# Key loads between z's weights, gate weights two rooms on, five PSUM banks for the delta rule: one decoder layer on one core

## The chip, the core and the metric

The kernel runs on one core of a Trainium2 chip. The metric is device time in microseconds, the median of three runs: 2111.9 us before the change (2111.68 to 2111.97). In the profile PE is TensorE, DVE is VectorE, ACT is ScalarE, POOL is GpSimd and SP is the engine whose queue issues nearly all loads and stores here.

## The reference

One layer of a hybrid decoder, 1024 tokens of width 1024, all in float32:

```python
x = layer_norm(a * x + 0.5 * swiglu(x, ffn1_wg, ffn1_wu, ffn1_wd), ln1_g, ln1_b)
proj = x @ w_in                       # q, k, v, z, b, a of 4 delta heads; q, keys, values, gates of 8 NSA heads
o_gdn = gdn_mixer(...)                # short causal conv, silu, l2norm, gated delta rule, rms norm * silu(z)
o_nsa = nsa_mixer(...)                # compressed + selected (top 16 of 16 blocks of 64) + window (512) attention
x = layer_norm(a * x + concat(o_gdn, o_nsa) @ w_out, ln2_g, ln2_b)
x = layer_norm(a * x + 0.5 * swiglu(x, ffn2_wg, ffn2_wu, ffn2_wd), ln3_g, ln3_b)

swiglu = (silu(x @ wg) * (x @ wu)) @ wd      # hidden width 2816
```

## The kernel before

All float32 products are made of three matmuls: each operand is split into a high part (a cast on ScalarE, `wh`, `xh`) and a low part (a subtraction on VectorE, `wl`, `xl`), and high x high, high x low and low x high add up in one PSUM bank. A bank holds 128 x 512 values; there are eight.

The stages in order, with their times in the profile:

- First FFN, `hidden` (to about 430): gate and up weights come in pairs of 128-column blocks (`load`, L247 to L260: a megabyte per weight and pair, into a ring of three rooms, `wring`, L197). Each pair's two products, one of 1024 x 1024 by 256 each, are made by Strassen-like schemes of seven products of half size (`Unit`, `prep` casts a weight, `run` L299 multiplies). Pair 0 takes rooms 0 and 1, four tiles of x that are set aside (`xf`) take room 2. For pair 0 the work is written out by hand up to L540, and pair 1's weights are loaded at L520 within it. The hand-written order holds for VectorE, ScalarE and POOL (in the second FFN for TensorE too). Sums of weights are `st`; L526 and L527 add up pair 0's products and so free their banks.
- Down projection (430 to 655), L642, into two sets of four banks.
- `project`, which holds the PSUM pools `pps` (products) and `gps` (all of the delta rule's banks, `bank`, L1308). `ln_first` transposes the normed rows (L122, `tp`, in banks of `gps`) into `xh`, `xl`; then eight blocks of q, k and v follow, each with a product of two halves (L173, 24 matmuls per half) and a causal convolution (`conv_block`, ScalarE copies each half out of PSUM at L841). The first two blocks' first halves are made before their second halves.
- `nat_block` (L958) and beside it the generator `gdn_couple`, which prepares the delta rule for eight chunks of 128 tokens. Per chunk `front` transposes q and k (L1341, two banks), and `back` transposes `lb` (L1415), makes a decay (L1419, L1421) and two halves of k against k and q (L1434); VectorE reads `lb`'s bank at L1426 (`zb`), and the others at L1436 and L1437. Product matmuls of other blocks (L173) stand between.
- `gdn_run` (from about 907), then `attend`: tiles of sparse attention (L1752, L1753, L1689), with the generator `z_blocks` between them, which makes z's eight products (L1083) one piece at a time. Its weights `zw`, half a megabyte per half block, come through two buffers: when four of a block's eight steps are done, the load of the next block's half goes out (L1061). Within the first block, `z_blocks` also issues the loads of the second head group's keys, `ks`, for two branches (selected, window) and two halves (`nsa_keys`, L1655: two loads of 256 KB each).
- Second FFN (from about 1440) and its down projection.

Instructions that aren't under a hand-written order are placed by a scheduler that goes by the program's order, by data and by free buffers. A room, a bank or a buffer is free when its last reader is done. SP issues its queue in order; an issue that has to wait holds all behind it.

Of the kernel before, what the change touches and what calls it, by code (L numbers as in the profile page):

```python
# [9 lines left out]
F32 = mybir.dt.float32  # L10
F32R = mybir.dt.float32r
# [5 lines left out]
PSUM = bass.MemoryType.PSUM  # L17

P = 128
# [28 lines left out]
class Layer:  # L48
# [135 lines left out]
    def hidden(self, wg, wu, hd, cols, halves, rows, extra, jobs):  # L184
        nc, tc = self.nc, self.tc
        eng = mybir.EngineType
        h0, h1 = halves
        with ExitStack() as st:


            def pool(n, **kw):
                return st.enter_context(tc.tile_pool(name=n, reuse_waits="tile", **kw))
# [4 lines left out]
            wring = Ring(*[(pool(f"fw{i}", bufs=1), "wraw") for i in range(3)])  # L197
# [49 lines left out]
            def load(w, p, parts=1):  # L247
                raw = wring.tile([P, ND, 2 * P], F32, "wraw")
                src = w[:, 2 * p * P:2 * (p + 1) * P].rearrange("(k p) f -> p k f", p=P)
                n = ND // parts  # L250

                def part(i):
                    nc.sync.dma_start(raw[:, i * n:(i + 1) * n], src[:, i * n:(i + 1) * n])

                if parts == 1:
                    part(0)
                    return raw
                return raw, part
# [139 lines left out]
            with tc.manual_schedule(engines=engines):  # L398
# [86 lines left out]
                def ready(n, src, vals, between=None):  # L485

                    w = [g.prep(src(g))]
                    for kc in range(4):
                        put(n, kc, vals[kc])
                    if between is not None:  # L490
                        between()
                    return w + [v.prep(src(v))]

                def go(i, n, w, k=None):
                    for u, x in zip(both, w):
                        u.p[i] = u.run(x, n, k)
# [20 lines left out]
                room("t4", h0)  # L517
                go(4, "t4", ready("t4", lambda u: u.w22, T))

                nxt = Gate(load(wg, 1)), Up(load(wu, 1))  # L520
                n = nxt[0]
                for x, w in (("x11", n.w11), ("x21", n.w12)):
# [446 lines left out]
    def project(self, ln_g, ln_b, w_in, a_log, dt_bias, pos_k, pos_v, k_w1, k_w2, v_w1, v_w2, outer):  # L969
        tc = self.tc  # L970
        self.w_in = w_in
        self.qkvT = self.scratch("qkvT", [12, P, T])
        self.zT = self.scratch("zT", [4, P, T])
        self.qd = self.scratch("qd", [HQ, P, T])
        self.kd = self.scratch("kd", [2, 2, P, T])
        self.cd = self.scratch("cd", [2, P, T])
        self.od = self.scratch("od", [GH, P, T])
        self.gts = self.mid.tile([P, NT, 32], F32, name="gts")
        self.KC = self.mid.tile([P, 2, 2, DH], F32R, name="KC")
        self.VC = self.mid.tile([DH, 2, 2, DH], F32R, name="VC")  # L980
        with ExitStack() as st:

            p1, p2 = [st.enter_context(tc.tile_pool(name=f"pw{i}", bufs=1, reuse_waits="tile")) for i in range(2)]
            self.raws, self.his, self.los = Ring((p1, "r0"), (p1, "r1"), (p2, "r2")), Ring((p1, "h0"), (p2, "h1")), Ring((p1, "l0"), (p2, "l1"))
            self.sb = st.enter_context(tc.tile_pool(name="psb", bufs=1, reuse_waits="tile"))
            with ExitStack() as ps:
                self.ps = ps.enter_context(tc.tile_pool(name="pps", bufs=4, space=PSUM, reuse_waits="tile"))
                self.pg = ps.enter_context(tc.tile_pool(name="gps", bufs=4, space=PSUM, reuse_waits="tile"))
                ws = [self.weights(w_in, 4 * P)]
                with tc.tile_pool(name="ln", bufs=4, reuse_waits="tile") as lsb:  # L990
                    scale = self.ln_first(lsb, self.pg, ln_g, ln_b)

                    ws.append(self.weights(w_in, 5 * P))
                    pps = [self.product(self.ps, "pr", *w, halves=(0,)) for w in ws]
                    for w, pp in zip(ws, pps):
                        self.product(self.ps, "pr", *w, halves=(1,), ps=pp)
                    for t, b in enumerate((4, 5, 6, 7, 0, 1, 2, 3)):
                        self.conv_block(b, pps[t] if t < 2 else None)
                        scale(t)
                couple = self.gdn_couple(a_log, dt_bias)  # L1000
                self.nat_block(couple)
                for _ in couple:
                    pass
                with tc.tile_pool(name="gc", bufs=1, reuse_waits="tile") as c1, tc.tile_pool(name="gb", bufs=2, reuse_waits="tile") as gb:
                    self.gdn_run(c1, gb)
                self.c_block(0, C_KC)
                self.c_block(1, C_VC)
                self.k_block(0, C_KS)
                self.k_block(1, C_KW)
                self.KS = {}  # L1010
                for br in range(2):
                    for half in (1, 0):
                        self.nsa_keys(0, br, half, self.acc_tile(2 * half + br, [P, 2, 512], F32R))
                self.nsa_consts()
                self.q_block(0)
                self.q_block(1)
                finish = self.cmp_mlp(0, pos_k, k_w1, k_w2, False)
                self.q_block(2)
                finish()
                finish = self.cmp_mlp(1, pos_v, v_w1, v_w2, True)  # L1020
                self.q_block(3)
                finish()


    def attend(self):
        nc, tc = self.nc, self.tc
# [3 lines left out]
        with ExitStack() as st:  # L1030
# [17 lines left out]
            def load_w(u):  # L1048

                for i, x in enumerate((self.xh, self.xl)):  # L1050
                    x[u] = self.xp[2 * i + u].tile([P, ND, 512], F32R, name=("xh", "xl")[i])
                for k in (4, 6, 0, 2):
                    for i, x in enumerate((self.xh, self.xl)):
                        loads.append(lambda i=i, x=x[u], k=k: nc.sync.dma_start(
                            x[:, k:k + 2, :].bitcast(F32), self.wo[i, u, k:k + 2].rearrange("k p c -> p k c")))

            def z_blocks():

                def load(n, k):
                    w = op.tile([P, 2, 4, P], F32R, name="zw", tag=("oh", "ol")[k], bufs=1)  # L1060
                    nc.sync.dma_start(w.bitcast(F32), self.zw[n % 4][:, k].rearrange("p i (k f) -> p i k f", f=P))  # L1061
                    return w

                w = [load(0, k) for k in range(2)]

                def finish(u, b, pp):
                    z = zp.tile([P, 512], F32, name="z", padded_shape=[P, T])

                    def out():
                        nc.scalar.mul(z, z, self.nw)  # L1070
                        nc.sync.dma_start(self.zT[b][:, u * 512:u * 512 + 512], z)

                    return [lambda: nc.scalar.activation(z, pp, AF.Tanh), lambda: None,
                            lambda: nc.vector.scalar_tensor_tensor(z, z, 1.0, pp, op0=ALU.add, op1=ALU.mult), out]

                for n in range(8):
                    u, b = divmod(n, 4)
                    pp = self.zps.tile([P, 512], F32, name="pr")
                    for kc in range(ND):
                        h, l = [w[kc // 4][:, i, kc % 4] for i in range(2)]  # L1080
                        xh, xl = self.xh[u][:, kc, :], self.xl[u][:, kc, :]
                        for i, (a, x) in enumerate(((h, xh), (h, xl), (l, xh))):
                            nc.tensor.matmul(pp, a, x, start=(kc == 0 and i == 0), stop=(kc == ND - 1 and i == 2))  # L1083
                        if kc % 4 == 3 and n < 7:
                            w[kc // 4] = load(n + 1, kc // 4)
                        yield
                        if n == 0 and kc in (3, 5):
                            for br in range(2):
                                self.nsa_keys(1, br, kc // 5, nk.tile([P, 2, 512], F32R, name=f"ks{br}{kc // 5}"))
                    if b == 3:  # L1090
                        load_w(u)
                    for f in finish(u, b, pp):
                        f()
                        yield
# [125 lines left out]
            with tc.manual_schedule(engines={eng.PE}):  # L1220
# [7 lines left out]

                nxt = group(0)
                filler.append(z_blocks())  # L1230
                for t in reversed(range(NT)):
                    if t + 2 < NT:
# [634 lines left out]
```

## Time and profile before

| | us |
|---|---|
| median of three runs | 2111.9 |
| the profiled run | 2113.0 |
| its span | 2111.2 |
| TensorE busy | 2064.5 (98%) |
| VectorE busy | 1508.6 (71%) |
| ScalarE busy | 922.5 (44%) |
| POOL busy | 586.6 (28%) |

The span runs from the first to the last instruction of one profiled execution; the granted TensorE clock is 0.996 over it. Times of the trace are counted from the span's start. "Granted clock" is the share of 2.4 GHz that the throttle granted; 0.5 is 1.2 GHz. An engine's row "idle before" names what ended its idle time.

### The profile page before, as it was taken

The page shows a single profiled execution, that of the slowest core. Times are in us where ns is not written, and L with a number is a line of the kernel's source. Part 1 is how long each engine was busy: PE and PEld are TensorE (multiplying, and loading weights), DVE is VectorE, ACT ScalarE, POOL GpSimd, SP SyncE. Part 2 cuts the span into 40 slices and gives each one's busy share as a digit, 9 for nine tenths or more (in the row PEclk, how much of TensorE's full clock was granted, in tenths as well). Part 3 has the DMA queues.
Part 4 walks back from the last instruction along what each step waited for, and adds up shares of the span by engine and source line. Part 5 has one row for each costly group of instructions (what it writes and reads, how often), then busy time and mean ns, then how long its engine had stood idle before and what let it go on. Part 6 is the DMA issues. An engine that isn't in the chain of part 4 may idle for free.

```text
span 2111.2 us, 29640 instructions
## 1 busy us (share of the span) xinstructions
PE 2064.5 (98%) x10247; PEld 1707.3 (81%) x10247; DVE 1508.6 (71%) x2644; ACT 922.5 (44%) x1957; POOL 586.6 (28%) x608
## 2 busy tenths in 40 slices
PE   9999999999999999999999999999999999999998
PEld 7788888888888897788877777787788888887886
DVE  7876767688877747735556777766976566569998
ACT  6333333344443434244446766656433333334441
POOL 2544445200021113000013354452254453310011
PEclk9999999999999999999999999999999999999999
DMA  4345555198623724477554421222333233259751
GB/s 147 123 147 178 200 185 180 71 334 278 230 69 95 232 93 152 136 220 199 143 145 170 163 73 50 72 85 81 110 105 120 95 111 102 73 219 328 235 195 55
DMA packets 251384, 316.46 MB, mean 150 GB/s; under 512 B 25393, under 2 KB 154530, under 8 KB 251234
## 3 DMA queue, kind: packets, MB, share of 16 engines
q1 hardware_dynamic: 246498, 298.05, 43.6%
q0 software_dynamic: 4736, 16.52, 2.0%
q8 instruction: 81, 1.33, 0.3%
q14 instruction: 69, 0.57, 0.1%
HBM read 219.08 MB, written 93.32 MB: 148 GB/s over the span
## 4 chain that ended last, share of the span: by engine, by line
PE 79%; DVE 8%; DMA 4%; issue 3%; POOL 2%; ACT 2%; SPq 1%; POOLq 0%; DVEq 0%; ACTq 0%
PE bk L299 34%; PE dn L642 17%; PE pr L173 9%; PE pr L1125 3%; PE po L1689 3%; PE pt L1676 2%; PE pr L1083 2%; PE pr L958 1%; DMA raw<-h 1%; PE sc L1753 1%; PE sc L1752 1%; DVE wl L285 1%; PE ga L1528 1%; PE ga L1538 1%; DVE st L278 1%
## 5 line engine op out<-in xcount | busy, mean ns | idle before, releaser
L299 PE MATMUL bk<-x,wh 128*128 128x512 f32 x1040 | 321.4, 390 | 4.9 <-DVE ev L527 2.8
L642 PE MATMUL dn<-bl,ah 128*128 128x512 f32 x616 | 240.3, 390 | 1.5 <-DVE bl L103 1.5
L642 PE MATMUL dn<-bh,ah 128*128 128x512 f32 x616 | 240.0, 390 | 0.2 <-DVE ev L320 0.2
L642 PE MATMUL dn<-bh,al 128*128 128x512 f32 x616 | 239.8, 389 | 0.0
L299 PEld LDWEIGHTS bk<-x,wh 128*128 128x128 f32 x1040 | 194.4, 188 | 47.0 <-issue 4.1
L299 PE MATMUL bk<-t,wh 128*128 128x512 f32 x704 | 217.1, 389 | 0.3 <-DVE t L240 0.3
L299 PE MATMUL bk<-acc,wh 128*128 128x512 f32 x704 | 217.0, 389 | 0.4 <-ACT ev L233 0.2
L284 ACT CAST wh<-st 128x512 fp32r<-128x512 f32 x176 | 108.3, 622 | 239.0 <-PE bk L299 202.9
L299 PE MATMUL bk<-x,wl 128*128 128x512 f32 x520 | 202.6, 390 | 2.1 <-DVE wl L285 2.0
L100 ACT CAST ah<-raw 128x512 fp32r<-128x512 f32 x154 | 95.3, 622 | 175.5 <-PE dn L642 94.3
L356 POOL TENSOR_TENSOR ev<-ev 128x512 f32<-128x512 f32 x80 | 131.6, 1647 | 144.5 <-ACT wh L284 65.7
L284 ACT CAST wh<-wraw 128x512 fp32r<-128x512 f32 x130 | 80.2, 623 | 186.5 <-PE bk L299 172.3
L1786 POOL TENSOR_SCALAR pr<-pr,f 128x512 f32<-128x512 f32 (+3 forms) x192 | 108.1, 582 | 176.6 <-DMA ks<-kd 36.2
L299 PEld LDWEIGHTS bk<-t,wh 128*128 128x128 f32 x704 | 132.1, 188 | 28.2 <-DVE t L240 0.8
L1757 DVE TENSOR_REDUCE nm<-sc 128x1 f32<-128x512 f32 (+3 forms) x192 | 98.2, 517 | 79.3 <-PE sc L1755 75.1
L299 PEld LDWEIGHTS bk<-acc,wh 128*128 128x128 f32 x704 | 132.0, 188 | 28.2 <-ACT ev L233 0.4
L278 POOL TENSOR_TENSOR st<-wraw 128x512 f32<-128x512 f32 x76 | 100.9, 1328 | 183.0 <-DVE wl L285 153.8
L285 DVE TENSOR_TENSOR wl<-wraw,wh 128x512 fp32r<-128x512 f32 x130 | 117.4, 907 | 37.7 <-ACT wh L284 36.5
L1758 ACT ACTIVATE pr<-sc,nm 128x512 f32<-128x512 f32 (+3 forms) x192 | 106.3, 555 | 72.0 <-DVE nm L1757 63.9
L642 PEld LDWEIGHTS dn<-bl,ah 128*128 128x128 f32 x616 | 115.6, 188 | 26.9 <-DVE bl L103 3.6
L299 PE MATMUL bk<-t,wl 128*128 128x512 f32 x352 | 137.0, 389 | 0.0
L299 PE MATMUL bk<-acc,wl 128*128 128x512 f32 x352 | 136.9, 389 | 0.0
(398 smaller groups left out, 4793.7 us busy)
## 6 DMA issues: line engine op xcount, KB each, us to landing
raw<-h SPq DMA_DIRECT2D x154, 256.0 KB
raw<-in_ffn_wd_dram SPq DMA_DIRECT2D x154, 256.0 KB
h<-ev SPq DMA_DIRECT2D x140, 256.0 KB
wraw<-in_ffn_wg_dram SPq DMA_DIRECT2D x20, 1024.0 KB
wraw<-in_ffn_wu_dram SPq DMA_DIRECT2D x20, 1024.0 KB
wraw<-in_w_in_dram SPq DMA_DIRECT2D x20, 512.0 KB
acc<-in_x_dram SPq DMA_DIRECT2D x32, 256.0 KB
wo<-ev SPq DMA_DIRECT2D x32, 256.0 KB
```

The lines of the kernel that those rows point to most:

```text
L100: nc.scalar.copy(hi, src)
L173: nc.tensor.matmul(ps[half], ws[:, kc, :], xs[half][:, kc, :], start=(kc == 0 and i == 0), stop=(kc == ND - 1 and i == 2))
L278: (e or u.adder).tensor_tensor(t, a, b, op=o)
L284: nc.scalar.copy(h, src)
L285: u.low = nc.vector.tensor_tensor(l, src, h.bitcast(F32), op=ALU.subtract)
L299: nc.tensor.matmul(ps, w[:, kc, :], v[kc], start=(kc == 0 and i == 0), stop=(kc == 3 and i == 2))
L356: (nc.vector if u.f + 2 == NF else nc.gpsimd).tensor_tensor(t, t, u.gate.g[i, j], op=ALU.mult)
L642: nc.tensor.matmul(ps, a[:, t * P:(t + 1) * P], w, start=start and i == 0, stop=stop and i == 2)
L1125: nc.tensor.matmul(pp, a[:, kc, :], w[u][:, kc, :], start=(kc == ks[0] and i == 0), stop=(kc == ks[-1] and i == 2))
L1757: nc.vector.tensor_reduce(nm[:, j, h:h + 1], ps[:, :w], axis=AX.X, op=ALU.max, negate=True)
L1758: return lambda: nc.scalar.activation(prs[j][:, h, :], ps[:, :w], AF.Exp, bias=nm[:, j, h:h + 1], accum_out=sm[:, j, h:h + 1])
L1786: nc.gpsimd.tensor_scalar(prs[j][:, h, :], prs[j][:, h, :], f[:, j, h:h + 1], 1.0, op0=ALU.mult, op1=ALU.mult)
```

## The change

There are three parts. First, `hidden` steps the ring of rooms on by two before pair 1's weights are loaded, in both FFNs: pair 1's gate weights get room 2, its up weights room 0, pair 2's gate weights room 1. Second, `pps` has three banks and `gps` five; the second half of the second block's product takes a bank of `gps`. Third, the four pairs of `ks` loads stand at four steps of z's blocks: behind step 5 of block 0, steps 1 and 5 of block 1, step 1 of block 2.

```diff
--- before.py
+++ after.py
@@ -517,6 +517,8 @@
                 room("t4", h0)
                 go(4, "t4", ready("t4", lambda u: u.w22, T))
 
+                for _ in range(2):
+                    next(wring.rooms)
                 nxt = Gate(load(wg, 1)), Up(load(wu, 1))
                 n = nxt[0]
                 for x, w in (("x11", n.w11), ("x21", n.w12)):
@@ -984,14 +986,17 @@
             self.raws, self.his, self.los = Ring((p1, "r0"), (p1, "r1"), (p2, "r2")), Ring((p1, "h0"), (p2, "h1")), Ring((p1, "l0"), (p2, "l1"))
             self.sb = st.enter_context(tc.tile_pool(name="psb", bufs=1, reuse_waits="tile"))
             with ExitStack() as ps:
-                self.ps = ps.enter_context(tc.tile_pool(name="pps", bufs=4, space=PSUM, reuse_waits="tile"))
-                self.pg = ps.enter_context(tc.tile_pool(name="gps", bufs=4, space=PSUM, reuse_waits="tile"))
+                self.ps = ps.enter_context(tc.tile_pool(name="pps", bufs=3, space=PSUM, reuse_waits="tile"))
+                self.pg = ps.enter_context(tc.tile_pool(name="gps", bufs=5, space=PSUM, reuse_waits="tile"))
                 ws = [self.weights(w_in, 4 * P)]
                 with tc.tile_pool(name="ln", bufs=4, reuse_waits="tile") as lsb:
                     scale = self.ln_first(lsb, self.pg, ln_g, ln_b)
 
                     ws.append(self.weights(w_in, 5 * P))
-                    pps = [self.product(self.ps, "pr", *w, halves=(0,)) for w in ws]
+                    pps = [[self.ps.tile([P, 512], F32, name="pr") for _ in range(n)] for n in (2, 1)]
+                    pps[1].append(self.bank().rearrange("p a b -> p (a b)"))
+                    for w, pp in zip(ws, pps):
+                        self.product(self.ps, "pr", *w, halves=(0,), ps=pp)
                     for w, pp in zip(ws, pps):
                         self.product(self.ps, "pr", *w, halves=(1,), ps=pp)
                     for t, b in enumerate((4, 5, 6, 7, 0, 1, 2, 3)):
@@ -1062,6 +1067,7 @@
                     return w
 
                 w = [load(0, k) for k in range(2)]
+                keys = {(0, 5): (0, 0), (1, 1): (1, 0), (1, 5): (0, 1), (2, 1): (1, 1)}
 
                 def finish(u, b, pp):
                     z = zp.tile([P, 512], F32, name="z", padded_shape=[P, T])
@@ -1084,9 +1090,10 @@
                         if kc % 4 == 3 and n < 7:
                             w[kc // 4] = load(n + 1, kc // 4)
                         yield
-                        if n == 0 and kc in (3, 5):
-                            for br in range(2):
-                                self.nsa_keys(1, br, kc // 5, nk.tile([P, 2, 512], F32R, name=f"ks{br}{kc // 5}"))
+
+                        if (n, kc) in keys:
+                            br, k = keys[n, kc]
+                            self.nsa_keys(1, br, k, nk.tile([P, 2, 512], F32R, name=f"ks{br}{k}"))
                     if b == 3:
                         load_w(u)
                     for f in finish(u, b, pp):
```

On SP, in the first FFN: `wraw_669` and `wraw_671` are pair 1's gate and up weights, `wraw_1007` and `wraw_1009` pair 2's. Before:

```order
L363 DMA h1_126<-ev_421 128x512
L253 DMA wraw_1007<-in_ffn1_wg_dram 128x8x256
L253 DMA wraw_669<-in_ffn1_wg_dram 128x8x256
L253 DMA wraw_671<-in_ffn1_wu_dram 128x8x256
L363 DMA h1_126<-ev_698 128x512
L363 DMA h1_126<-ev_322 128x512
L253 DMA wraw_1009<-in_ffn1_wu_dram 128x8x256
```

Here the gate weights of pair 2 go out first. The same place of SP's queue after the change:

```order
L363 DMA h1_126<-ev_421 128x512
L253 DMA wraw_669<-in_ffn1_wg_dram 128x8x256
L253 DMA wraw_671<-in_ffn1_wu_dram 128x8x256
L253 DMA wraw_1007<-in_ffn1_wg_dram 128x8x256
L363 DMA h1_126<-ev_698 128x512
L363 DMA h1_126<-ev_322 128x512
L253 DMA wraw_1009<-in_ffn1_wu_dram 128x8x256
```

Pair 1's two loads now stand ahead of pair 2's gate weights; the second FFN has the same move.

On SP, at the start of the attention: `ks` are the key loads (two each), `zw` z's weights, `zT` the write of a z block, `qs` a load of queries. Before:

```order
L1061 DMA zw<-zw 128x1024
L1666 DMA qs<-qd 128x4x128
L1655 DMA ks_10040<-kd 64x2x512 x2
L1655 DMA ks_10043<-kd 64x2x512 x2
L1655 DMA ks_10057<-kd 64x2x512 x2
L1655 DMA ks_10060<-kd 64x2x512 x2
L1061 DMA zw<-zw 128x1024
L1071 DMA zT<-z 128x512
L1061 DMA zw<-zw 128x1024 x2
```

All four pairs of `ks` go out one behind the other. The same place of SP's queue after the change:

```order
L1066 DMA zw<-zw 128x1024
L1673 DMA qs<-qd 128x4x128
L1662 DMA ks_10051<-kd 64x2x512 x2
L1066 DMA zw<-zw 128x1024
L1077 DMA zT<-z 128x512
L1662 DMA ks_10138<-kd 64x2x512 x2
L1066 DMA zw<-zw 128x1024
L1662 DMA ks_10167<-kd 64x2x512 x2
L1066 DMA zw<-zw 128x1024
L1077 DMA zT<-z 128x512
L1662 DMA ks_10230<-kd 64x2x512 x2
```

A load of `zw` now stands behind each pair of `ks`, where all four pairs stood ahead of it.

On TensorE, in the preparation of the delta rule, from the halves of chunk 0 (L1434, after: L1441) over the transposes of chunk 2 (L1341, after: L1348) into chunk 1's back: `pr` are product matmuls of another block. Before:

```order
L1434 MATMUL ga<-kq 128x256 x4
L1341 MATMUL ga<-ident,kq 128x128 x8
L173 MATMUL pr<-xl,wh 128x512
L173 MATMUL pr<-xh,wl 128x512
L1415 MATMUL ga<-ident,lb 128x128 x4
L173 MATMUL pr<-xh,wh 128x512
L1419 LDWEIGHTS identb
L1419 MATMUL ga<-m_below,identb 128x512
L1421 MATMUL ga<-ut,lg 128x128 x4
L173 MATMUL pr<-xl,wh 128x512
L173 MATMUL pr<-xh,wl 128x512
L173 MATMUL pr<-xh,wh 128x512
```

Product matmuls stand between the steps of chunk 1's back. The same place on TensorE after the change:

```order
L1441 MATMUL ga<-kq 128x256 x4
L1348 MATMUL ga<-ident,kq 128x128 x8
L1422 MATMUL ga<-ident,lb 128x128 x4
L1426 LDWEIGHTS identb
L1426 MATMUL ga<-m_below,identb 128x512
L1428 MATMUL ga<-ut,lg 128x128 x4
L1441 MATMUL ga<-kq 128x256 x4
L173 MATMUL pr<-xl,wh 128x512
L173 MATMUL pr<-xh,wl 128x512
L173 MATMUL pr<-xh,wh 128x512
L173 MATMUL pr<-xl,wh 128x512
```

The product matmuls that stood between the steps of chunk 1's back now stand behind its last step.

## Rows read from the trace of the kernel before

**Rows 1.** The page's first part: busy time of each engine in the span, its share and its instructions.
```profile
PE 2064.5 (98%) x10247; PEld 1707.3 (81%) x10247; DVE 1508.6 (71%) x2644; ACT 922.5 (44%) x1957; POOL 586.6 (28%) x608
```

**Rows 2.** The table by stretches. Columns: the stretch, its length, then busy time and instructions of PE, PEld, DVE, ACT and POOL, the granted TensorE clock as a share of full speed, the busy share of the DMA engines, and GB/s.
```profile
45.00:65.00 20.00, 17.77 (x82) 13.86 (x80) 16.78 (x28) 10.50 (x19) 1.29 (x1) 1.00 0.49 159
...
672.00:765.00 93.00, 93.00 (x468) 80.00 (x467) 66.78 (x85) 31.86 (x51) 11.15 (x18) 1.00 0.60 193
...
765.00:860.00 95.00, 89.80 (x494) 76.40 (x493) 60.95 (x129) 41.92 (x162) 23.86 (x19) 0.98 0.40 128
...
1070.00:1100.00 30.00, 24.84 (x121) 18.76 (x120) 13.91 (x39) 14.15 (x39) 6.03 (x10) 0.94 0.67 187
...
1485.00:1530.00 45.00, 41.09 (x184) 32.59 (x183) 41.84 (x64) 20.15 (x34) 10.68 (x8) 1.00 0.39 129
```

**Rows 3.** The list of waits of TensorE from 1070 to 1100: engine, operation and line, what it waited for and at which line; us in total, times, the longest.
```profile
PE pr L1083 <- DMA zw<-zw: 4.2, 1, 4.2
```

**Rows 4.** The timeline of SP's DMA queue from 1070 to 1092: start, us, queue, line, operation, out<-in, and how many in a run (their us together).
```profile
1071.84 5.19 SPq L1655 DMA_DIRECT2D ks<-kd  x8
1077.13 0.54 SPq L1061 DMA_DIRECT2D zw<-zw  x1
...
1080.54 9.94 SPq L1061 DMA_DIRECT2D zw<-zw  x2
```

**Rows 5.** The timeline of TensorE from 1072 to 1102, the same columns, with the idle time before a row and what ended it in brackets.
```profile
1072.22 0.39 PE L1083 MATMUL pr<-xh,zw 128*128 128x512 f32 x1
...
1079.19 0.40 PE L1083 MATMUL pr<-xl,zw 128*128 128x512 f32 x1
...
1080.52 0.23 PE L1755 MATMUL sc<-m_upto,identb 128*128 128x128 bf16 x1
...
1084.92 0.50 PE L1083 MATMUL pr<-xh,zw 128*128 128x512 f32 x1 [4.17 <-DMA zw<-zw]
...
1087.91 0.63 PE L1083 MATMUL pr<-xl,zw 128*128 128x512 f32 x1
...
1092.04 0.50 PE L1083 MATMUL pr<-xh,zw 128*128 128x512 f32 x1 [0.19 <-DVE z L1074]
...
1101.63 0.48 PE L1752 MATMUL sc<-ks,qs 128*128 128x512 f32 x1
```

**Rows 6.** The table by stretches, columns as in rows 2, of the two places where the granted clock falls.
```profile
799.10:802.40 3.30, 3.30 (x15) 2.81 (x13) 3.30 (x5) 2.48 (x17) 0.00 (x0) 0.50 0.70 240
1085.60:1088.80 3.20, 3.20 (x12) 2.58 (x11) 0.29 (x1) 0.46 (x2) 0.36 (x1) 0.53 0.09 37
```

**Rows 7.** What the DMA engines moved from 1070 to 1092, in 40 slices of 0.55 us each, GB/s.
```profile
GB/s 119 313 305 209 97 263 257 285 257 235 250 246 209 235 257 238 238 242 235 242 235 250 238 246 313 380 447 402 350 30 0 0 0 0 0 0 0 0 89 134
```

**Rows 8.** TensorE's waits for zb from 765 to 860, columns as in rows 3, and out of the timelines of TensorE and VectorE the longest of them and the zb that ended it.
```profile
PE ga L1341 <- DVE zb L1426: 3.1, 3, 1.8
PE ga L1419 <- DVE zb L1426: 1.6, 1, 1.6
...
797.77 0.66 PE L1341 MATMUL ga<-ident,kq 128*128 128x128 f32 x4 [1.81 <-DVE zb L1426]
...
797.02 0.69 DVE L1426 TENSOR_TENSOR zb<-ga,dk 128x512 f32<-128x512 f32 x1
```

**Rows 9.** The first FFN from 45 to 60: SP's timeline (two issues in one row), a piece of the chain that ended last (start, us, what), and the timelines of VectorE and TensorE.
```profile
46.15 5.19 SPq L253 DMA_DIRECT2D wraw<-in_ffn_wg_dram  x2
...
50.97 5.40 DMA wraw<-in_ffn_wg_dram
...
53.25 0.70 DVE L285 TENSOR_TENSOR wl<-wraw,wh 128x512 fp32r<-128x512 f32 x1
...
57.10 1.29 DVE L285 TENSOR_TENSOR wl<-wraw,wh 128x512 fp32r<-128x512 f32 x2 [3.15 <-ACT wh L284]
...
59.02 0.69 DVE L527 TENSOR_TENSOR ev<-ev,bk 128x512 f32<-128x512 f32 x1
...
59.86 0.70 PE L299 MATMUL bk<-x,wh 128*128 128x512 f32 x2 [1.66 <-DVE ev L527]
```

**Rows 10.** The second FFN from 1490 to 1530: SP's timeline, the piece of the chain, VectorE's list of waits, and the timelines of TensorE and VectorE.
```profile
1491.09 5.19 SPq L253 DMA_DIRECT2D wraw<-in_ffn_wg_dram  x2
...
1495.90 5.18 DMA wraw<-in_ffn_wg_dram
...
DVE wl L285 <- ACT wh L284: 3.1, 2, 2.9
...
1504.58 0.70 PE L299 MATMUL bk<-x,wh 128*128 128x512 f32 x2 [1.10 <-DVE ev L527]
...
1526.80 0.50 PE L299 MATMUL bk<-x,wl 128*128 128x512 f32 x1 [2.04 <-DVE wl L285]
...
1526.06 1.28 DVE L285 TENSOR_TENSOR wl<-wraw,wh 128x512 fp32r<-128x512 f32 x2
```

**Rows 11.** The stage of the first layer norm and the products behind it: TensorE's timeline at 626 and 656, ScalarE's at 697, TensorE's at 698.
```profile
626.14 1.91 PE L122 MATMUL tp<-ident,acc 128*128 128x128 f32 x16
...
656.78 1.31 PE L122 MATMUL tp<-ident,acc 128*128 128x128 f32 x10 [1.29 <-POOL acc L769]
...
697.09 1.05 ACT L841 COPY xp<-pr 128x512 f32<-128x512 f32 x2
...
698.62 0.39 PE L173 MATMUL pr<-xh,wh 128*128 128x512 f32 x1
```

## The prediction

> **What bounds the kernel now.** First the line of busy times: TensorE is busy 2064.5 of 2111.2 us, the others far less [rows 1]. So a change can save what TensorE idles, 46.7 us in all, and what it loses where its clock is granted at half. Next the table by stretches tells where that is [rows 2]: in the stages that the change touches TensorE idles 2.2 us (45 to 65), 5.2 us (765 to 860), 5.2 us (1070 to 1100) and 3.9 us (1485 to 1530); from 672 to 765 it never idles. The granted clock is below 1 only in the second and third of these. Then, for each, the list of what TensorE waited for, the chain, and the timeline of the engine that it waited for.
>
> **Keys, expected gain 5.4 us.** SP issues the eight loads of ks one behind the other from 1071.84 to 1077.03, and only then, at 1077.13, the load of zw that holds the second half of z's second block [rows 4]. TensorE is through with what it has at 1080.75 and stands 4.17 us, until 1084.92, for that load [rows 3, 5]. The transfer itself is not the trouble: meanwhile the DMA engines drain some 240 GB/s for the ks [rows 7], and 8 x 256 KB take about 9 us at that rate, from 1073 to 1082; zw's packets come behind them. Of its 7.8 us from issue to use, then, 4.9 are spent behind them and 2.9 are its own. Right after the wait the granted clock is about 0.5 for some 3.3 us, the 1.2 GHz level [rows 6]; a matmul lasts 0.63 us there against 0.40 [rows 5]. At half the clock 3.3 us of work cost 1.7 us more than at 2.4 GHz. Together 5.9 us.
>
> After the change only two ks loads stand ahead of that zw. Its buffer is free then: the matmuls of z's first block, which read it last, are issued by 1072.22 [rows 5]. Two issues of 0.65 us behind 1071.84 put zw at 1073.1, 4.0 us earlier. The 0.5 MB ahead of it are drained 2.1 us after 1073, and with its own 2.9 us it lands near 1078. That is before 1080.75: nothing is waited for, and nothing makes the clock fall there. What is late next: each remaining pair of ks (0.5 MB, 2.1 us of the queue) now stands before a later zw. The next zw goes out once its buffer is free, at 1080.54 [rows 4], and is wanted when z's third block starts: 1092.04 before [rows 5], 5.9 us earlier after, so 5.6 us after its issue. I charge 0.5 us for these. Bounds: all three pairs make the next zw late by their 2.1 us each, 6.3 us, which leaves -0.4; or none, 5.9. I take 5.4, near the upper end, because 2.1 us of queue and its own 2.9 us still fit into these 5.6. The ks themselves are first read at 1101.63 [rows 5], long after the first pairs' new issues.
>
> **Rooms, expected gain 4.6 us.** In both FFNs SP issues pair 2's gate weights first, into the room that comes free first, and pair 1's 4.8 us later, since pair 1 was given a room that is still read (46.15 and 50.97) [rows 9]. These land 5.4 us on, VectorE stands 3.15 us for ScalarE's cast of them, and TensorE 1.66 us for VectorE's L527, which releases a bank. After the change pair 1's gate weights take the early room, its up weights the one at 50.97, pair 2's gate weights the late one. So the cast can start near 51.6 in place of 56.45; VectorE is done with its preceding work at 53.95 and goes on without a stop: L527 is over 3.15 us earlier, at 56.5, and TensorE, which runs out at 58.2, finds its bank. Gain 1.7 us, and 0.1 of the small idles around it [rows 2], 1.8 us. In the second FFN the same pieces read: 1491.09, 1495.90 with 5.18 us, VectorE idle 2.9 us, TensorE idle 1.10 us, and then, because VectorE waits for nothing else that counts until 1526, once more 2.04 us for a wl at 1526.06 [rows 10]. With VectorE 2.9 us ahead that wl is ready at 1523.8, and TensorE, which wanted it at 1524.76 and is 1.10 us ahead, at 1523.7. Gain 1.1 + 2.0 = 3.1 us. Sum 4.9; I take 4.6, since VectorE also reads products of TensorE's in this stretch. Pair 2's gate weights, now last, have pair 1's 14 products of 12 matmuls ahead of them, 38 us at 0.23 us each. Bounds: 0 if another operand is as late, 4.9.
>
> **Banks, expected gain 2.5 us.** The delta rule's preparation waits for its four banks: 3.1 + 1.6 us are put down to zb at L1426, which reads one and so frees it [rows 8], of the 5.2 us idle there [rows 2]. Behind the longest piece, 1.81 us at 797.77, the clock is at half for 3.3 us [rows 6, 8], 1.7 us of loss. Together 6.9 us. A fifth bank lets TensorE go one step further, and the product matmuls that stood between the steps of one chunk now stand behind them. They still cover, only later. But the step after it waits on the same VectorE work: zb (0.69 us, at 797.02) has one for dk of the same size ahead of it, and a wait lasts at most these two, 1.4 us. Following the new order with the durations of before, three later steps get to a bank before its zb has read it, by 1.25, 0.95 and about 0.6 us, 2.8 in all; 6.9 - 2.8 = 4.1. I take 1.6 off, nearly the price of one half-clock stretch, since those waits may bring one. Bounds: the most is 6.9; at the other end five chunks that now run without product matmuls between wait 1.81 us each, 9.1 us, less the 5.2 that go: -3.9.
>
> Three product banks in place of four: from 672 to 765 each half of a product takes 24 matmuls, 5.5 us, and its bank is free once ScalarE's copy is done. The tightest: the first of two copies at 697.09 ends about 697.6, and the matmul that needs its bank comes at 698.62 [rows 11], 1 us of slack. The transposes at 626 to 632 now all stand behind the last down-projection matmul. They are the same 32 (16 of them take 1.91 us), so that matmul ends some 3.5 us earlier, and they run where TensorE stood 1.29 us for POOL [rows 11]. What ends this stage is VectorE's and POOL's chain on either side. I set it at 0, bounds -1.5 to +1.5.
>
> **Sum.** 5.4 + 4.6 + 2.5 + 0 = 12.5 us off the profiled run of 2113.0 us (span 2111.2), so 2100.5; that run lies 1.1 us above the median of 2111.9, so the forecast for the median is 2099.4 us.
>
> **A rule that speaks against it.** Two idle pieces, of 1.81 and 4.17 us, stand just before a fall of the granted clock [rows 5, 6, 8]; behind those of 1.66 and 2.04 us it stays at 1 [rows 2, 9, 10]. The Trainium skill ("TensorE: Matmul & The Clock Gate", A second HAM failure mode: psum-queue depth-cycling) says that a kernel which cycles through PSUM banks can idle in small pieces between groups of matmuls, often enough for the clock to swing. By that rule the new order of the preparation would lose more clock than I count; by the rows, with a fall behind two pieces of four, I count one. What it would give here is the last rival below.
>
> **The rivals.** (a) The wait for zw goes on to the next loads. For it: the DMA engines were full until 1082, and the ks must be moved anyway. Against: each pair now has some 3 us of slack. The keys give nothing: 2104.8. (b) The banks lose what their lower bound says, -3.9 in place of +2.5: 2105.8. For it: VectorE is the one that frees banks, and it is full. (c) The new room does nothing, as VectorE or TensorE's own products are late anyway: 2104.0. Against: the idle time named ScalarE's cast, and the cast the DMA. (d) Slower: seven of the eight chunks of the preparation, now without product matmuls between their steps, wait 1.81 us each and then run 3.3 us at half clock, as happened at 797.77: 7 x 3.5 = 24.5 us against the 6.9 that go, 17.6 more. With the other gains of 10.0 it ends at 2119.5. It decides from five such chunks on (16.9 / 3.5 = 4.8 even out). Against it: of the four waits for zb before [rows 8], one had a fall behind it.
>
> **How the numbers follow.** Forecast 0.68 (its own range 2095 to 2103: keys 3 to 5.9, rooms 3 to 4.9, banks 0 to 6); (a) 0.11; (b) 0.09; (c) 0.07; (d) 0.05. The range 2095 to 2107 takes in (a) to (c). A change within 0.2% (4.2 us) can't be told from none: from 2107.7 on. Faster 0.89: forecast and (a) to (c), less 0.06 where two of them come together; same 0.06; slower 0.05.
>
> **What would show it.** Keys: no wait of L1083 for zw near 1080, no half clock behind it; zw issued before the third ks. Rooms: pair 1's gate weights issued first at 46 and 1491, and no wait at 59.9, 1504.6 and 1526.8. Banks: waits for zb below 3 us from 765 to 860, and clock 1 there. Wrong it is if the list has a zw wait at a later block, or if the stretch from 765 to 860 idles over 5 us.

## The result, and the profile after

The changed kernel takes 2098.68 us (median of six runs, 2097.06 to 2100.8), the kernel before 2112.77 us on the same chips: a ratio of 0.9934, interval 0.9922 to 0.9947. 14.1 us went, 12.5 were forecast; 2099.4 us was the forecast time.

The profiled execution has a span of 2098.8 us. Its line of busy times [rows 1]:

```profile
PE 2061.0 (98%) x10247; PEld 1705.7 (81%) x10247; DVE 1515.8 (72%) x2644; ACT 922.9 (44%) x1957; POOL 588.8 (28%) x608
```

TensorE idles 37.8 us in place of 46.7, and it is busy 3.5 us less with the same instructions, about what the two half-clock stretches of [rows 6] cost, 1.7 us each. The table by stretches, the same places as in [rows 2], the fourth moved with the work (columns as there):

```profile
45.00:65.00 20.00, 19.58 (x94) 15.99 (x93) 19.93 (x34) 12.14 (x22) 2.71 (x3) 1.00 0.49 159
672.00:765.00 93.00, 93.00 (x470) 80.14 (x469) 66.12 (x85) 32.51 (x56) 11.12 (x18) 1.00 0.60 194
765.00:860.00 95.00, 91.86 (x510) 78.48 (x509) 62.58 (x132) 42.12 (x160) 24.10 (x19) 1.00 0.40 128
1065.00:1095.00 30.00, 29.02 (x155) 22.43 (x154) 17.91 (x45) 17.69 (x48) 9.66 (x16) 1.00 0.72 200
1485.00:1530.00 45.00, 44.40 (x196) 36.41 (x196) 44.93 (x57) 17.83 (x31) 20.66 (x14) 1.00 0.40 132
```

The granted clock is 1 in all of them. TensorE idles 0.4, 0, 3.1, 1.0 and 0.6 us there, against 2.2, 0, 5.2, 5.2 and 3.9. In the fifth stretch, which was not moved, 0.6 us of waits for ScalarE now lie ahead of 1485; from 1475 to 1520 TensorE idles 1.3 us. What is left, by the list of waits of 765 to 860, of 1065 to 1095 and of 1485 to 1530:

```profile
PE ga L1422 <- DVE zb L1433: 2.9, 2, 1.6
PE ga L1426 <- DVE QK L1444: 0.2, 1, 0.2
...
PE pr L1089 <- DVE z L1080: 1.0, 2, 0.8
...
PE bk L299 <- DVE wl L285: 0.6, 1, 0.6
```

SP's queue at the keys, to be read against [rows 4]: zw is issued behind the first pair of ks, and no wait for zw is left.

```profile
1067.34 1.29 SPq L1662 DMA_DIRECT2D ks<-kd  x2
1068.67 0.59 SPq L1066 DMA_DIRECT2D zw<-zw  x1
1071.67 0.33 SPq L1077 DMA_DIRECT2D zT<-z  x1
1072.04 1.25 SPq L1662 DMA_DIRECT2D ks<-kd  x2
1076.18 0.33 SPq L1066 DMA_DIRECT2D zw<-zw  x1
```

The first FFN, SP's and VectorE's timelines, against [rows 9]. The gate weights of pair 1 now go out first, the three wl of L285 run through without a stop, and L529 (L527 before) comes 1.8 us earlier, although this execution began 1.5 us later (1.2 us of it arise by 16 us, with a granted clock of 0.50 from 11 to 15 us, where the kernel before had 1.00):

```profile
47.63 0.38 SPq L253 DMA_DIRECT2D wraw<-in_ffn_wg_dram  x1
52.44 0.38 SPq L253 DMA_DIRECT2D wraw<-in_ffn_wu_dram  x1
55.45 0.37 SPq L253 DMA_DIRECT2D wraw<-in_ffn_wg_dram  x1
...
54.74 1.88 DVE L285 TENSOR_TENSOR wl<-wraw,wh 128x512 fp32r<-128x512 f32 x3
...
57.26 0.69 DVE L529 TENSOR_TENSOR ev<-ev,bk 128x512 f32<-128x512 f32 x1
```

For a sum over the stages I matched every VectorE and ScalarE instruction of a trace with the same one of the trace of before, and took the median difference of their starts in a stretch; the step from one stretch to the next is what the stage between gained (minus) or lost, in us. What a trace has at 40 us, up to 1.5 us either way in all runs, is where its execution began and is left out.

| stage | changed kernel | again (E11) | keys alone (E1) | banks alone (E2) | again (E10) | rooms alone (E3) | no keys (E7) | no rooms (E8) |
|---|---|---|---|---|---|---|---|---|
| first FFN (45 to 430) | -2.4 | -2.4 | -0.4 | -0.3 | -0.3 | -2.3 | -2.4 | -0.3 |
| its down projection (to 626) | +0.5 | -0.2 | -0.5 | +0.9 | +0.9 | -0.1 | +0.3 | +0.4 |
| layer norm, products (to 765) | -0.4 | -0.4 | 0.0 | -0.3 | -0.3 | +0.1 | -0.3 | -0.4 |
| preparation (to 907) | -4.0 | -3.1 | 0.0 | -3.1 | -4.0 | 0.0 | -3.1 | -4.0 |
| delta rule (to 1075) | +0.5 | -0.5 | 0.0 | +1.5 | +0.6 | +0.4 | +1.1 | +0.4 |
| keys (to 1092) | -6.0 | -6.0 | -6.0 | +0.3 | -0.2 | -0.5 | +1.2 | -6.0 |
| second FFN's first pair (1490 to 1540) | -3.2 | -3.2 | 0.0 | -0.1 | +0.1 | -3.2 | -3.1 | +0.1 |

Behind 1540 the traces differ by up to 1.1 us either way (the changed kernel +1.1, E7 -1.0, E3 0), though no part of the change stands there. One execution of E1 took 7314.7 us and is left out of its median below.

### The profile page after: what moved, and what is told of

The parts are those of the page before. It is cut to its first block, busy times and chain, and to the rows that moved or that the text cites. A ratio compares the mean times of both kernels' runs of the same rounds, so it can differ in the third digit from the quotient of the medians.

```text
span 2098.8 us, 29633 instructions
## 1 busy us (share of the span) xinstructions
PE 2061.0 (98%) x10247; PEld 1705.7 (81%) x10247; DVE 1515.8 (72%) x2644; ACT 922.9 (44%) x1957; POOL 588.8 (28%) x608
## 4 chain that ended last, share of the span: by engine, by line
PE 83%; DVE 6%; issue 4%; DMA 3%; ACT 2%; POOL 2%; SPq 0%; POOLq 0%; DVEq 0%; ACTq 0%
PE bk L299 35%; PE dn L644 17%; PE pr L173 9%; PE pr L1132 3%; PE po L1696 3%; PE pt L1683 3%; PE pr L1089 2%; PE sc L1760 1%; PE sc L1759 1%; PE pr L960 1%; PE ga L1535 1%; DVE wl L285 1%; PE ga L1545 1%; DMA Y<-Yd 1%; DMA raw<-h 1%
## 5 line engine op out<-in xcount | busy, mean ns | idle before, releaser
L285 DVE TENSOR_TENSOR wl<-wraw,wh 128x512 fp32r<-128x512 f32 x130 | 122.7, 948 | 31.5 <-ACT wh L284 30.4
L110 POOL TENSOR_TENSOR rstd<-rstd,mhalf 128x1 f32<-128x1 f32 x24 | 22.2, 929 | 411.3 <-DVE rstd L108 411.1
```

Source lines behind the costliest of these rows:

```text
L285: u.low = nc.vector.tensor_tensor(l, src, h.bitcast(F32), op=ALU.subtract)
```

## The experiments

### The three parts alone

E1 has only the new places of the key loads, E2 only the banks (with the second block's second half in a bank of `gps`, as in the change), E3 only the rooms:

```diff
E1, in z_blocks
+                keys = {(0, 5): (0, 0), (1, 1): (1, 0), (1, 5): (0, 1), (2, 1): (1, 1)}
...
-                        if n == 0 and kc in (3, 5):
...
+                        if (n, kc) in keys:
E2, in project
-  name="pps", bufs=4 ...  name="gps", bufs=4
+  name="pps", bufs=3 ...  name="gps", bufs=5
E3, in hidden
+                for _ in range(2):
+                    next(wring.rooms)
```

Expected, E1: 

> Only the key loads are placed as in the change. Theory (queue): zw's packets wait behind the keys' packets, so this part alone takes away the wait of 4.17 us near 1080 and the half clock behind it (1.7 us): VectorE's and ScalarE's instructions behind 1092 come 5.5 to 6.0 us earlier than in the kernel before, and the end too, ratio 0.9972. Rival (the wait goes on): a zw wait of 2 us or more appears at a later z block, and the end gains less than 4 us, ratio above 0.998.

Expected, E2: 

> Only the banks are split three and five. Theory (five banks let TensorE run ahead of VectorE in the preparation): about nothing up to 765, 3.5 to 4.5 us gained between 765 and 870, half a microsecond lost again up to 1060, no granted clock below 1 from 765 to 860; the end about 3.5 us earlier, ratio 0.9983. Rival (the gain in the changed kernel came from another part's shift of the times, for example of loads): less than 2 us gained between 765 and 870, and the fall of the clock near 800 is still there.

Expected, E3: 

> Only the rooms are stepped on by two. Theory (the room dates pair 1's gate weights): the waits at 59.9, 1504.6 and 1526.8 in TensorE's list go, 1.8 us at the first place and 3.1 us at the second, and some of it is given back in the down projections, as in the changed kernel: the end 3 to 4 us earlier, ratio 0.9984. Rival (all of it is given back, since another chain sets the end of each FFN): the end within 1 us, ratio above 0.9995.

Measured: E1 2105.59 us, ratio 0.9966 (0.9953 to 0.9979); E2 2110.32, 0.9987 (0.9979 to 0.9996); E3 2107.3, 0.9974 (0.9965 to 0.9983), with 2112.56 for before. The shares that go, 0.34, 0.13 and 0.26%, add up to 0.73%, against 0.66% (0.53 to 0.78) for all three together: within the noise, no part needs another.

E1 gains its 6.0 us at the one place and nothing elsewhere, as the queue theory has it; no zw wait comes at a later block. E2 gains 3.1 us in the preparation, less than the 3.5 to 4.5 expected, and gives back 1.5 us, more than the half microsecond expected, while the fall of the clock near 800 is gone. E3 gains 5.5 us at the two FFNs' heads and gives next to nothing back; I had expected 3 to 4 us, reading too much into a microsecond that the changed kernel's trace loses in its down projections. E1's and E2's own down projections lie -0.5 and +0.9 us from before without any change to them, so that microsecond belongs to no part.

### How long zw waits behind the keys (E4, E9)

E4 puts three pairs ahead of that zw, E9 two; the change has one, the kernel before four. Both are shown against E1.

```diff
-                keys = {(0, 5): (0, 0), (1, 1): (1, 0), (1, 5): (0, 1), (2, 1): (1, 1)}
+                keys = {(0, 3): (0, 0), (0, 4): (1, 0), (0, 5): (0, 1), (2, 1): (1, 1)}
...
+                keys = {(0, 3): (0, 0), (0, 5): (1, 0), (1, 5): (0, 1), (2, 1): (1, 1)}
```

Expected, E4: 

> As the keys alone, but three of the four pairs of key loads stand ahead of that zw and one behind it. Queue theory: SP issues zw 1.3 us earlier than before (1075.8), 1.5 MB of keys are drained by 1079.5, zw's own part is 2.9 us, so it lands at 1082.4, and TensorE waits 1.7 us in place of 4.2. Rival (the time from issue to landing is fixed at 7.75 us, whatever stands ahead): it lands at 1083.5, a wait of 2.8 us. The clock: by the waits of the kernel before (falls behind 1.81 and 4.17, none behind 1.66 and 2.04) either is open; if the clock falls behind a wait of this size, the loss is again near 1.7 us.

Expected, E9: 

> As the keys alone, but two pairs of key loads stand ahead of that zw. Queue theory, with the size that three pairs showed: 1 MB of keys are drained 4.3 us after their first packet, zw's own part is 3.2 us, so it lands within 0.2 us of the moment when TensorE wants it (1080.75 by the times of before): a wait of 0 to 0.4 us, no fall of the clock, the end 5.5 to 6 us earlier. Rival (7.2 to 7.8 us from issue to landing in any case): a wait of 0.9 to 1.5 us.

In E4 TensorE waits 2.12 us; its timeline, and the table by stretches right behind it:

```profile
1081.01 0.50 PE L1089 MATMUL pr<-xh,zw 128*128 128x512 f32 x1 [2.12 <-DMA zw<-zw]
...
1081.00:1084.40 3.40, 3.39 (x18) 2.93 (x19) 0.58 (x2) 0.61 (x3) 3.09 (x5) 1.00 0.86 264
```

The wait lies nearer to the queue's 1.7 us than to the rival's 2.8, and the granted clock stays at 1: the stage gains 3.6 us, 2.05 of the wait, and the other 1.6 close to the 1.7 of the clock. In E9 no wait for zw is in the list, where a fixed time from issue to landing would have left 0.9 us or more; the stage gains 6.0 us like E1. Four, three, two and one pairs ahead of zw give waits of 4.2, 2.1, 0 and 0 us: that fits a price of 2.1 us of queue for a pair, as the sum had it, and the change has one pair to spare. The size is known roughly only: with four pairs other executions (E2, E3, E5, E7, E10) waited 3.6 to 4.15 us (E6, whose attention begins in another order, 2.45), and two pairs leave no wait to measure. (Single executions took 2107.21 us for E4 and 2110.19 for E9, whose trace lost 1.6 us of clock at another place, below.)

### Which weights date the FFN's wait (E5)

```diff
-                for _ in range(2):
+                for _ in range(1):
                     next(wring.rooms)
```

Expected: 

> Only the rooms, stepped on by one in place of two: SP then issues pair 1's up weights first (46), pair 2's gate weights second (51) and pair 1's gate weights last (54). Theory (the landing of pair 1's gate weights sets L526 and L527): they land 3.0 us later than before, so TensorE's wait for L527 grows from 1.66 to 4.7 us in the first FFN and from 1.10 to 4.1 us in the second, and the wait for wl in the second stays about 2.0; the end 5 to 9 us later than before (the upper figure if the clock falls behind both waits). Rival (VectorE's other work or the up weights set it): the waits stay near 1.7 and 1.1.

SP's timeline in the first FFN, and TensorE's timeline and the table by stretches behind the wait in the first and the second:

```profile
44.83 0.38 SPq L253 DMA_DIRECT2D wraw<-in_ffn_wu_dram  x1
49.64 3.38 SPq L253 DMA_DIRECT2D wraw<-in_ffn_wg_dram  x2
...
61.34 1.19 PE L299 MATMUL bk<-x,wh 128*128 128x512 f32 x2 [4.46 <-DVE ev L529]
...
1510.28 1.19 PE L299 MATMUL bk<-x,wh 128*128 128x512 f32 x2 [4.18 <-DVE ev L529]
...
61.30:64.70 3.40, 3.36 (x8) 2.71 (x9) 3.37 (x6) 2.10 (x4) 0.23 (x1) 0.51 0.00 0
1510.30:1513.70 3.40, 3.40 (x8) 2.72 (x9) 3.37 (x6) 2.12 (x4) 0.30 (x1) 0.50 0.00 0
```

The waits are 4.46 and 4.18 us, as the theory had them (4.7 and 4.1), and the clock falls behind both. 2118.07 us in one execution against 2114.74, 3.3 us more, where 5 to 9 were expected; counted from 40 us the trace ends 6.4 us later than the one of before. The landing of pair 1's gate weights sets L529. The wait of 2.0 us for wl, which I expected to stay, is gone from the list of this kernel: TensorE has fallen back 5.0 us behind L529's wait, and VectorE 3.1, so that VectorE is in time.

### The price of a product bank (E6)

```diff
-  name="pps", bufs=4 ...  name="gps", bufs=4
+  name="pps", bufs=2 ...  name="gps", bufs=6
...
+                    pps[1] += [self.bank().rearrange("p a b -> p (a b)") for _ in range(2)]
```

Expected: 

> Only the banks, two for products and six for the delta rule (both halves of the second block's first product stand in the delta rule's banks). If five banks still were the limit in the preparation, the waits for zb of 2.9 + 0.9 us that are left with five fall to under 1.5 us. If they are set by VectorE's pace, they stay above 2.5 us. Price of a product bank: with three the tightest matmul has 1 us of slack, with two it wants its bank 5.5 us earlier, so TensorE waits 4 us and more for ScalarE's copies near 693, and again in the following blocks; rival (the copies come early enough): under 1 us of new waits between 672 and 765.

TensorE's waits of 672 to 765 and of 765 to 860:

```profile
PE pr L173 <- ACT xp L843: 4.5, 1, 4.5
...
PE ga L1426 <- DVE zb L1433: 3.4, 2, 2.1
PE ga L1441 <- DVE zb L1433: 1.0, 1, 1.0
```

One wait of 4.5 us stands where three banks had 1 us of slack, and with the fall of the clock behind it the stage loses 6.0 us; the blocks behind it have enough room with two banks as well. In the preparation the sixth bank takes nothing away: 4.4 us for zb against 2.9 to 3.8 with five. With five banks it is VectorE's pace that is waited for, no longer the number of banks. One of E6's waits for zb, of 2.10 us at 808.39, has a fall of the clock behind it. (A single execution: 2119.29 us. Its trace also loses 5.9 us between 907 and 1075, where a wait of 1.66 us for `qs` at 1056.89 has half clock behind it, and gets 3.8 back at the keys, so the total is not the price of a product bank.)

### Two of three parts, and two repeats (E7, E8, E10, E11)

E7 is the changed kernel with the key loads of before, E8 with the rooms of before; E10 repeats E2, E11 the changed kernel.

Expected, E7: 

> The changed kernel with the key loads as before (banks and rooms changed). If the parts add up: the wait of 4.2 us for zw and the half clock behind it are back, the end 6.0 us later than in the changed kernel, so 7 to 8 us faster than before, ratio 0.9965. The preparation, 765 to 870: 4.0 us gained if it depends on what came before it as in the changed kernel, 3.1 us if as with the banks alone.

Expected, E8: 

> The changed kernel with the rooms as before (banks and keys changed). If the parts add up: the waits at 59.9, 1504.6 and 1526.8 are back, 5.5 us, and the end is 7 to 9 us faster than before, ratio 0.9962. The preparation, 765 to 870, as with the banks alone: 3.1 us gained, with a wait of 0.9 us for zb in the products of k with k and q; if 4.0 us again, the difference was chance and not the rooms.

Expected, E10: 

> The banks alone once more. If the wait of 0.9 us for zb in the products of k with k and q, and the half microsecond more or less that waits for Y cost, are chance from execution to execution, one of the two comes out otherwise than in the first run of this kernel: 765 to 870 gains 4.0 us, or the waits for Y are not 2 of 1.2 us. If they belong to the kernel, 3.1 us and 1.2 us again.

Expected, E11: 

> The changed kernel once more. If the difference to the banks alone in the preparation (4.0 against 3.1 us gained from 765 to 870) is chance, either figure can come; the places of keys and rooms show the same waits as in its first run, none at 59.9, 1504 and 1080, and 0.6 us near 1513.

E7 2104.38 us, ratio 0.9948 (0.9932 to 0.9965); E8 2104.67, 0.9951 (0.9936 to 0.9966), with 2114.74 for before; both expected ratios, 0.9965 and 0.9962, lie at the upper ends of these intervals. E7's preparation gains 3.1 us and E8's 4.0, but not for what stands before it: the repeats swap the two figures. In E2, E7 and E11 the list has one wait more than in the changed kernel's first run, E8 and E10, although E10 has the code of E2, and E11 that of the changed kernel. E2's list first, then E10's:

```profile
PE ga L1422 <- DVE zb L1433: 2.9, 2, 1.6
PE ga L1441 <- DVE zb L1433: 0.9, 1, 0.9
PE ga L1426 <- DVE QK L1444: 0.2, 1, 0.2
```

```profile
PE ga L1422 <- DVE zb L1433: 2.9, 2, 1.6
PE ga L1426 <- DVE QK L1444: 0.2, 1, 0.2
```

So 0.9 us in the preparation is chance from execution to execution; what decides it I did not find. E5, with four banks, also comes out 0.9 us better than before at that place, without any change there. In E7 the wait for zw is back, and it costs more than before: behind 4.15 us the clock is at half for longer than in [rows 6].

```profile
1079.39 0.79 PE L1089 MATMUL pr<-xh,zw 128*128 128x512 f32 x1 [4.15 <-DMA zw<-zw]
...
1079.40:1082.80 3.40, 3.40 (x10) 2.82 (x11) 0.00 (x0) 0.00 (x0) 1.04 (x2) 0.50 0.25 102
1082.80:1086.20 3.40, 3.40 (x13) 2.60 (x13) 0.58 (x2) 1.30 (x5) 0.00 (x0) 0.62 0.00 0
```

3.40 x 0.50 + 3.40 x 0.38 = 3.0 us are lost in these two stretches alone, against 1.7 before. This is why E7, which lacks the keys, lost 1.2 us against before at that place.

## Why the prediction was right, point by point

The time, the sign and the three mechanisms held: the sum of 12.5 us stands against 14.1 us of medians and 13.9 us between the two profiled executions when both are counted from 40 us. In both runs of the changed kernel each of the three parts gave somewhat more than its term. The terms:

- **Keys**, forecast 5.4: 6.0 us in every run that has them (E1, E8, the changed kernel twice). The wait of 4.17 and the clock's 1.7 both went. The 0.5 us charged for the later zw loads did not come. Rival (a), the wait that goes on to the next load, is out: no zw wait in any of these runs. The step "a pair is 2.1 us of queue" agrees with E4 and E9.
- **Rooms**, forecast 1.8 + 3.1, taken as 4.6: 2.3 or 2.4 and 3.2, 5.5 to 5.6 us in the four runs that have them. The second FFN came as worked out: of the 1.10 us none is left, of the 2.04 us 0.6. Both places give some 0.6 us more than the waits that went (1.8 and 2.5); where that comes from is open. Rival (c) is out by E3 and E5.
- **Banks**, forecast 2.5 with bounds from -3.9 to 6.9: the preparation gained 3.1 to 4.0. "Waits of 2.8 us in all" stand against 3.1 to 4.0 measured, so the 1.2 to 2.1 us of idle time that went are less than the 2.4 of the sum. The step "a wait lasts at most these two, 1.4 us" did not hold: the longest is 1.6 to 1.7. The clock, for which I kept back 1.6, did not fall in six runs with five banks, and that is the term that was mis-sized. What I left out is the other side: up to 1.5 us are lost again in the delta rule behind it, so that the net is 1.6 to 3.6 us. The runs without a change there scatter by 0.4 us either way at that stage. The lists show a wait for the load of Y there, 1.0 to 2.0 us with five banks, 0.5 to 1.3 with four; that it makes the loss was not tried, and it can't be all of it: E8 waits 1.9 us for Y and loses 0.4, E2 2.0 and loses 1.5.
- **Three product banks**, forecast 0: no wait between 672 and 765. The slack of 1 us was real, as E6 shows from the other side.
- **The transposes behind the down projection**, forecast 0: -0.3 to -0.4 us. The idle 1.29 us became three pieces of 0.2 to 0.4.
- **Rival (d)**, chunks that wait 1.8 us and then lose the clock, did not come: none of the pieces of 0.9 to 1.7 us that five banks leave in the preparation had a fall behind it in six runs. The Trainium skill ("TensorE: Matmul & The Clock Gate", A second HAM failure mode: psum-queue depth-cycling) says that small idle pieces between matmul groups can swing the clock. The traces agree for single pieces, of 1.81 us with four banks (four executions of six) and of 2.10 us with six (E6); a clock that swings again and again is in none of them.
- **The signs named ahead** held in part for the waits: zb below 3 us in the changed kernel's first run (2.9), not in its repeat E11 (3.8), and of the wait at 1526.8 0.6 us are left.

The sum for the banks also added the 1.7 us of clock to the idle time as if the two were independent, and they are not. In E9 and E4, with four banks, the clock did not fall in the preparation; TensorE was 1.45 us ahead behind that place and then waited for a fourth zb, where [rows 8] has three at that line. E9's list from 765 to 860:

```profile
PE ga L1348 <- DVE zb L1433: 4.0, 4, 1.8
```

Of the 1.7 us only 0.35 were left at 907: VectorE's pace took back most of what the clock gave.

The probabilities were stated with 0.11 for (a), for which nothing was left once zw's own 2.9 us were subtracted; that could have been read from the trace of before.

## What to carry over

A load that something waits for belongs ahead of loads that nobody needs yet; count the bytes that stand ahead of it in the queue, and divide by the rate that the trace shows there. Where a ring of rooms is shared, look at the order in which the rooms come free, not at the order in which the program names them. And price a wait of TensorE with the clock that it loses: behind the nine waits of 3.5 us and more here that was about a third to three quarters on top, as an estimate from half the time at half clock. Where another engine sets the pace behind the wait, as VectorE does in the preparation, most of that loss is no gain when it goes.

## What the runs showed of the hardware

The same wait does not always cost the same clock. The piece of 1.81 us in the preparation with four banks stands before a fall in the kernel before and in E1, E3 and E5, and before none in E4 and E9. First E1, then E4, the stretch right behind it:

```profile
796.20:799.60 3.40, 3.12 (x17) 2.65 (x18) 3.40 (x7) 1.30 (x11) 0.00 (x0) 0.73 0.40 134
799.60:803.00 3.40, 3.40 (x15) 2.88 (x15) 3.40 (x5) 2.65 (x10) 1.64 (x1) 0.77 0.81 244
```

```profile
796.70:800.10 3.40, 3.12 (x21) 2.54 (x22) 3.39 (x7) 1.29 (x11) 0.00 (x0) 1.00 0.41 132
```

Four such pieces of six had a fall behind them, of the 2.0 us pieces at L285's wl in the second FFN two of eight (E6 and E9; it cost E9 1.6 us). All nine pieces of 3.5 us and more had one, and of those of 1.66 us and less behind the first 20 us just one, in E6. Length alone does not decide: in E6 the clock fell behind pieces of 1.66, 2.07 and 2.10 us and not behind one of 2.45 us for zw. After a wait of about 4 us at the keys the half clock cost 1.7 us in the kernel before, E3 and E10, and about 3 in E7; in E2 and E5 it was 2.7 and 2.9, by the same estimate. So the keys part is worth 5.9 us by the profiled execution of before, and some 7 by E7's.
